# A DoRA linear layer: 4 MB blocks with results written over the input rows, in place of 2 MB blocks with output buffers of their own

## The chip, the cores and the metric

The kernel runs on one core of one Trainium2 chip. The time is the device time of one execution in microseconds (us); the figure given for a kernel is the median over several runs.

## The reference

The input x has 16 x 2048 = 32,768 rows of 256 numbers (float32, 33.6 MB), and the output has the same shape. The weight is small: W (256 x 256) plus a low-rank term, each column scaled to length m.

```python
W_adapted = W + scale * (lora_A @ lora_B)          # rank 16
W_norm = np.sqrt(np.sum(W_adapted ** 2, axis=0, keepdims=True) + 1e-8)
W_final = W_adapted / W_norm * m
y = x.reshape(-1, in_dim) @ W_final
```

## The kernel before, in words

The start builds W_final once: four small loads, matmuls for A @ B and for the column norms (L116), a square root on ScalarE (L120), and multiplications on VectorE that end in `w_final`, written in two halves by L127. This part has a raised priority.

The main loop (L134) goes over 16 blocks of 2048 rows. A block is `x_sb`, 128 partitions with DJ = 16 rows of 256 float32 each; row p*16 + j of the block lies in partition p, so a partition's share is 16 KB in one piece in memory, and a load is 128 such pieces. L53 issues it from SP. A block is worked in groups of J = 4 row slots, c = 0 to 3, so 64 groups in all (call them groups 0 to 63, and the blocks 0 to 15). One group is:

- eight 128x128 transposes on TensorE (L142) from `x_sb` into `xt_ps` in PSUM;
- one cast to bf16 on VectorE (L148) into `xt_sb`;
- eight matmuls on TensorE (L153) with 256 columns of `w_final` into `y_ps`;
- one copy on ScalarE (L160) from `y_ps` into a slice of `y_sb`.

After the last group of a block, L162 issues its store from ACT's queue, `y_sb` to the output, again 16 KB per partition.

Buffers set how far the parts may run apart: six `x_sb`, five `y_sb`, six `xt_sb`, two `xt_ps`, two `y_ps`. A load may begin when the transposes of the block that used its buffer are done; a copy into `y_sb` when the store that used that buffer is done. The order of instructions on each engine is fixed when the program is built. A scheduler sets it, with its own notion of costs and of data arriving, so the order in which transposes and result matmuls alternate on TensorE is not the order of the source: transposes are put ahead by some groups.

Of the kernel before, what the change touches and what calls it, by code (L numbers as in the profile page):

```python
# [10 lines left out]
@with_exitstack  # L11
def kernel(
    ctx: ExitStack,
    tc: tile.TileContext,
    x: bass.AP,
    W: bass.AP,
    lora_A: bass.AP,
    lora_B: bass.AP,
    m: bass.AP,
    scale: float,  # L20
    out: bass.AP,
):
    nc = tc.nc
    P = 128
    FP32 = mybir.dt.float32
    BF16 = mybir.dt.bfloat16
    AF = mybir.ActivationFunctionType
    ALU = mybir.AluOpType

    x_flat = x.flatten_outer_dims()  # L30
    out_flat = out.flatten_outer_dims()
    N, IN = x_flat.shape
    OUT = W.shape[1]
    R = lora_A.shape[1]
    KC = IN // P
    J = 4
    DJ = 16
    BLK = DJ * P
    NBLK = N // BLK

    assert IN % P == 0 and OUT % P == 0 and N % BLK == 0

    consts = ctx.enter_context(tc.tile_pool(name="consts", bufs=1))
    startup = ctx.enter_context(tc.tile_pool(name="startup", bufs=1))
    xpool = ctx.enter_context(tc.tile_pool(name="xpool", bufs=6))
    xtpool = ctx.enter_context(tc.tile_pool(name="xtpool", bufs=6))
    ypool = ctx.enter_context(tc.tile_pool(name="ypool", bufs=5))
    pp_xt = ctx.enter_context(tc.tile_pool(name="pp_xt", bufs=2, space=bass.MemoryType.PSUM))
    pp_y = ctx.enter_context(tc.tile_pool(name="pp_y", bufs=2, space=bass.MemoryType.PSUM))

    def load_x(b):
        t = xpool.tile([P, DJ, IN], FP32, name="x_sb", tag="x_sb")
        nc.sync.dma_start(  # L53
            out=t,
            in_=x_flat[b * BLK : (b + 1) * BLK].rearrange("(p j) k -> p j k", p=P),
        )
        return t


    a_nat = startup.tile([P, KC, R], FP32)  # L60
    nc.scalar.dma_start(out=a_nat, in_=lora_A.rearrange("(c p) r -> p c r", p=P))
    w_nat = startup.tile([P, KC, OUT], FP32)
    nc.sync.dma_start(out=w_nat, in_=W.rearrange("(c p) o -> p c o", p=P))  # L63
    b_nat = startup.tile([R, OUT], FP32)
    nc.scalar.dma_start(out=b_nat, in_=lora_B)
    m_row = startup.tile([1, OUT], FP32)
    nc.scalar.dma_start(out=m_row, in_=m[None, :])

    identity = consts.tile([P, P], FP32)
    make_identity(nc, identity)  # L70
    ones = consts.tile([P, P], FP32)
    nc.vector.memset(ones, 1.0)
    eps_col = startup.tile([P, 1], FP32)
    nc.vector.memset(eps_col, 1e-8)

    warm = startup.tile([P, 1], FP32)
    nc.scalar.activation(out=warm, in_=eps_col, func=AF.Sqrt)  # L77

    w_final = consts.tile([P, KC, OUT], BF16)

    with tc.high_priority():
        b_bf = startup.tile([R, OUT], BF16)
        nc.vector.tensor_copy(out=b_bf, in_=b_nat)  # L83

        aT_ps = pp_y.tile([R, KC * P], FP32, tag="psy", name="aT_ps")
        for c in range(KC):
            nc.tensor.transpose(aT_ps[:, c * P : (c + 1) * P], a_nat[:, c, :], identity)  # L87
        aT = startup.tile([R, KC * P], BF16)
        nc.vector.tensor_copy(out=aT, in_=aT_ps)  # L89

        mb_ps = pp_y.tile([P, OUT], FP32, tag="psy", name="mb_ps")
        nc.tensor.matmul(mb_ps, ones[0:1, :], m_row, start=True, stop=True)  # L92
        m_all = startup.tile([P, OUT], FP32)
        nc.vector.tensor_copy(out=m_all, in_=mb_ps)  # L94

        ab_ps = pp_y.tile([P, KC, OUT], FP32, tag="psy", name="ab_ps")
        for c in range(KC):
            nc.tensor.matmul(  # L98
                ab_ps[:, c, :],
                aT[:, c * P : (c + 1) * P],  # L100
                b_bf,
                start=True,
                stop=True,
            )

        wa = startup.tile([P, KC, OUT], FP32)
        nc.vector.scalar_tensor_tensor(  # L107
            out=wa, in0=ab_ps, scalar=float(scale), in1=w_nat, op0=ALU.mult, op1=ALU.add
        )
        sq = startup.tile([P, KC, OUT], FP32)  # L110
        nc.vector.tensor_mul(out=sq, in0=wa, in1=wa)  # L111


        n2_ps = pp_y.tile([P, OUT], FP32, tag="psy", name="n2_ps")
        for c in range(KC):
            nc.tensor.matmul(  # L116
                n2_ps, ones, sq[:, c, :], start=(c == 0), stop=(c == KC - 1)
            )
        norm = startup.tile([P, OUT], FP32)
        nc.scalar.activation(out=norm, in_=n2_ps, func=AF.Sqrt, bias=eps_col)  # L120
        wam = startup.tile([P, KC, OUT], FP32)
        for c in range(KC):
            nc.vector.tensor_mul(out=wam[:, c], in0=wa[:, c], in1=m_all)  # L123
        rnorm = startup.tile([P, OUT], FP32)
        nc.vector.reciprocal(out=rnorm, in_=norm)  # L125
        for c in range(KC):
            nc.vector.tensor_mul(out=w_final[:, c], in0=wam[:, c], in1=rnorm)  # L127

    j_order = []
    for a in range(J // 2):  # L130
        j_order.append(a)
        j_order.append(a + J // 2)

    for b in range(NBLK):  # L134
        x_sb = load_x(b)
        y_sb = ypool.tile([P, DJ, OUT], FP32, name="y_sb")

        for c in range(DJ // J):
            xt_ps = pp_xt.tile([P, KC, J * P], FP32, tag="psxt", name="xt_ps")
            for j in range(J):  # L140
                for kc in range(KC):
                    nc.tensor.transpose(  # L142
                        xt_ps[:, kc, j * P : (j + 1) * P],
                        x_sb[:, c * J + j, kc * P : (kc + 1) * P],
                        identity,
                    )
            xt_sb = xtpool.tile([P, KC, J * P], BF16, name="xt_sb")
            nc.vector.tensor_copy(out=xt_sb, in_=xt_ps)  # L148

            y_ps = pp_y.tile([P, J, OUT], FP32, tag="psy", name="y_ps")  # L150
            for kc in range(KC):
                for j in j_order:
                    nc.tensor.matmul(  # L153
                        y_ps[:, j, :],
                        xt_sb[:, kc, j * P : (j + 1) * P],
                        w_final[:, kc, :],
                        start=(kc == 0 and (j % (J // 2)) == 0),
                        stop=(kc == KC - 1 and (j % (J // 2)) == (J // 2) - 1),
                    )
            nc.scalar.copy(out=y_sb[:, c * J : (c + 1) * J, :], in_=y_ps)  # L160

        nc.scalar.dma_start(  # L162
            out=out_flat[b * BLK : (b + 1) * BLK].rearrange("(p j) k -> p j k", p=P),
            in_=y_sb,
        )


# [33 lines left out]
```

## Time and profile before

| | |
|---|---|
| median of 8 runs | 165.92 us (165.60 to 166.53) |
| the profiled execution | 166.41 us, of which its span is 164.6 us |
| HBM read and written | 33.85 MB and 33.55 MB, 409 GB/s over the span |
| TensorE busy | 128.3 us (78%) |
| VectorE busy | 81.1 us (49%) |
| ScalarE busy | 63.9 us (39%) |
| one load: issue to landing | 2 MB, median 35.6 us |
| one store: issue to landing | 2 MB, median 15.7 us, shortest 8.1 |

The profile covers the execution on one core, from the first instruction to the last. The span is less than the time of the execution, as something lies around it. The page gives busy time by engine, then rows of 40 slices in which each digit is a busy share in tenths (the DMA row is the mean over 16 DMA engines), then the DMA queues with packets, megabytes and their share of the engines' time. PE is TensorE, PEld its weight loads, DVE VectorE, ACT ScalarE. A list of stretches gives, for each, its length, the busy time of PE, PEld, DVE, ACT and POOL with the instructions in it, TensorE's granted clock, the DMA share, and GB/s. A timeline lists instructions in order: start, duration, engine, line, operation, and in square brackets how long the engine had stood idle and what ended that.

### The profile page before, as it was taken

Reading aid. Unit: us, or ns where it says so; the run is one execution under the profiler, and the core shown is the slowest. Engines: PE = TensorE matmul, PEld = TensorE weight load, DVE = VectorE, ACT = ScalarE, POOL = GpSimd, SP = SyncE. Lnnn points to the kernel's source line nnn. Section 1 sums busy time; section 2 is a strip of 40 time slices with the busy share of each in tenths; the row PEclk is TensorE's granted clock in tenths of the full one; section 3 lists DMA queues with packets and bytes.
Section 4 is the critical chain, followed back from the end, with each engine's and each line's share of the span. In section 5 each row is a group of like instructions: output and inputs, shape, how many; then the busy total and the mean of one; then the engine's idle time right before and its main releaser. Section 6 shows DMA issues by size and latency. Waiting matters only on the chain.

```text
span 164.6 us, 2402 instructions
## 1 busy us (share of the span) xinstructions
PE 128.3 (78%) x1034; PEld 110.8 (67%) x1034; DVE 81.1 (49%) x76; ACT 63.9 (39%) x67; POOL 0.7 (0%) x6
## 2 busy tenths in 40 slices
PE   0495987989989898989898986989679894998300
PEld 0174876877867878787877876778577783897200
DVE  0198457569194646564646462564605555262000
ACT  3001742350714535353531714444406353268500
POOL 1000000000000000000000000000000000000000
PEclk9999999999999999999999997899978999999975
DMA  6999999999999999999999999999999999999991
GB/s 185 400 442 442 430 414 314 442 438 406 434 438 430 418 426 442 436 422 418 438 434 426 426 430 442 420 426 426 438 438 422 418 442 434 422 414 406 426 426 84
DMA packets 5196, 67.55 MB, mean 410 GB/s; under 512 B 817, under 2 KB 1090, under 8 KB 1090
## 3 DMA queue, kind: packets, MB, share of 16 engines
q1 hardware_dynamic: 2576, 33.82, 49.1%
q10 hardware_dynamic: 2610, 33.59, 48.0%
q8 instruction: 8, 0.13, 0.3%
q14 instruction: 2, 0.02, 0.0%
HBM read 33.85 MB, written 33.55 MB: 409 GB/s over the span
## 4 chain that ended last, share of the span: by engine, by line
PE 41%; DMA 34%; DVE 9%; ACT 6%; another core or an unknown queue 1%; issue 1%; SPq 0%
DMA x_sb<-in_x_dram 34%; PE xt_ps L142 20%; PE y_ps L153 20%; DVE xt_sb L148 8%; ACT y_sb L160 6%; DVE rnorm L125 1%; PE n_ps L116 1%; ACT norm L120 0%; SPq L63 0%
## 5 line engine op out<-in xcount | busy, mean ns | idle before, releaser
L148 DVE CAST xt_sb<-xt_ps 128x1024 bf16<-128x1024 f32 x64 | 75.6, 1219 | 59.6 <-PE y_ps L153 30.7
L160 ACT COPY y_sb<-y_ps 128x1024 f32<-128x1024 f32 x64 | 61.9, 1015 | 79.7 <-PE y_ps L153 70.0
L142 PE MATMUL xt_ps<-identity,x_sb 128*128 128x128 f32 x512 | 69.9, 284 | 15.1 <-DMA x_sb<-in_x_dram 9.5
L142 PEld LDWEIGHTS xt_ps<-identity,x_sb 128*128 128x128 f32 x512 | 59.1, 146 | 21.9 <-DVE xt_sb L148 20.4
L153 PE MATMUL y_ps<-w_final,xt_sb 128*128 128x256 bf16 x512 | 64.1, 276 | 3.7 <-ACT y_sb L160 2.7
L153 PEld LDWEIGHTS <-xt_sb 128*128 128x128 bf16 x512 | 50.6, 99 | 13.2 <-issue 5.6
L120 ACT ACTIVATE norm<-n_ps,eps_col 128x256 f32<-128x256 f32 x1 | 0.5, 475 | 8.7 <-PE n_ps L116 8.7
L87 PE MATMUL aT_ps<-identity,a_nat 128*16 128x128 f32 x2 | 0.6, 394 | 4.1 <-DMA a_nat<-in_lora_A_dram 4.1
L92 PE MATMUL mb_ps<-m_row,ones 1*128 1x256 f32 x2 | 1.2, 694 | 2.4 <-DMA m_row<-in_m_dram 2.4
L87 PEld LDWEIGHTS aT_ps<-identity,a_nat 128*16 128x16 f32 x2 | 0.1, 87 | 4.0 <-issue 4.0
L83 DVE CAST b_bf<-b_nat 16x256 bf16<-16x256 f32 x1 | 0.3, 282 | 5.0 <-DMA b_nat<-in_lora_B_dram 5.0
L92 PEld LDWEIGHTS mb_ps<-m_row,ones 1*128 1x128 f32 x2 | 0.5, 304 | 2.9 <-DVE aT L89 2.9
L77 ACT ACT_TABLE_LOAD x1 | 1.3, 1283 | 2.3 <-issue 2.3
L125 DVE RECIPROCAL rnorm<-norm 128x256 f32<-128x256 f32 x1 | 1.8, 1752 | 0.8 <-ACT norm L120 0.8
L116 PE MATMUL n_ps<-sq,ones 128*128 128x256 f32 x4 | 1.5, 516 | 0.0
L94 DVE COPY m_all<-mb_ps 128x256 f32<-128x256 f32 x1 | 0.4, 425 | 1.7 <-PE mb_ps L92 1.7
L116 PEld LDWEIGHTS n_ps<-sq,ones 128*128 128x128 f32 x4 | 1.1, 310 | 0.2
L123 DVE TENSOR_TENSOR wam<-wa,m_all 128x256 f32<-128x256 f32 x2 | 0.8, 420 | 0.0
L127 DVE TENSOR_TENSOR w_final<-wam,rnorm 128x256 bf16<-128x256 f32 x2 | 0.7, 411 | 0.0
L111 DVE TENSOR_TENSOR sq<-wa 128x512 f32<-128x512 f32 x1 | 0.7, 694 | 0.0
L107 DVE SCALAR_TENSOR_TENSOR wa<-ab_ps,w_nat 128x512 f32<-128x512 f32 x1 | 0.7, 692 | 0.0
L98 PE MATMUL ab_ps<-b_bf,aT 16*128 16x256 bf16 x2 | 0.6, 416 | 0.0
(11 smaller groups left out, 2.0 us busy)
## 6 DMA issues: line engine op xcount, KB each, us to landing
x_sb<-in_x_dram SPq DMA_DIRECT2D x16, 2048.0 KB, 35.6
out_dram<-y_sb ACTq DMA_DIRECT2D x16, 2048.0 KB, 15.7
w_nat<-in_W_dram SPq DMA_DIRECT2D x1, 256.0 KB, 3.0
a_nat<-in_lora_A_dram ACTq DMA_DIRECT2D x1, 16.0 KB, 3.2
b_nat<-in_lora_B_dram ACTq DMA_DIRECT2D x1, 16.0 KB, 4.7
m_row<-in_m_dram ACTq DMA_DIRECT2D x1, 1.0 KB
```

The lines of the kernel that those rows point to most:

```text
L77: nc.scalar.activation(out=warm, in_=eps_col, func=AF.Sqrt)
L87: nc.tensor.transpose(aT_ps[:, c * P : (c + 1) * P], a_nat[:, c, :], identity)
L92: nc.tensor.matmul(mb_ps, ones[0:1, :], m_row, start=True, stop=True)
L107: nc.vector.scalar_tensor_tensor(out=wa, in0=ab_ps, scalar=float(scale), in1=w_nat, op0=ALU.mult, op1=ALU.add)
L111: nc.vector.tensor_mul(out=sq, in0=wa, in1=wa)
L116: nc.tensor.matmul(n2_ps, ones, sq[:, c, :], start=(c == 0), stop=(c == KC - 1))
L123: nc.vector.tensor_mul(out=wam[:, c], in0=wa[:, c], in1=m_all)
L125: nc.vector.reciprocal(out=rnorm, in_=norm)
L142: nc.tensor.transpose(xt_ps[:, kc, j * P : (j + 1) * P], x_sb[:, c * J + j, kc * P : (kc + 1) * P], identity,)
L148: nc.vector.tensor_copy(out=xt_sb, in_=xt_ps)
L153: nc.tensor.matmul(y_ps[:, j, :], xt_sb[:, kc, j * P : (j + 1) * P], w_final[:, kc, :], start=(kc == 0 and (j % (J // 2)) == 0), stop=(kc ...
L160: nc.scalar.copy(out=y_sb[:, c * J : (c + 1) * J, :], in_=y_ps)
```

## The change

The number of row slots per block doubles, DJ from 16 to 32, so there are 8 blocks of 4096 rows and 4 MB, a block has eight groups (c = 0 to 7), and a partition's share of a load or a store is 32 KB in one piece. The separate output buffers go. ScalarE copies a group's result into the slice of `x_sb` that held the group's input rows, and the store reads from `x_sb`. There are five of these buffers; each is held from the load to the end of the store.

```diff
     J = 4
-    DJ = 16
+    DJ = 32
     BLK = DJ * P
...
-    assert IN % P == 0 and OUT % P == 0 and N % BLK == 0
+    assert IN == OUT and IN % P == 0 and OUT % P == 0 and N % BLK == 0
...
-    xpool = ctx.enter_context(tc.tile_pool(name="xpool", bufs=6))
+    xpool = ctx.enter_context(tc.tile_pool(name="xpool", bufs=5))
     xtpool = ctx.enter_context(tc.tile_pool(name="xtpool", bufs=6))
-    ypool = ctx.enter_context(tc.tile_pool(name="ypool", bufs=5))
...
         x_sb = load_x(b)
-        y_sb = ypool.tile([P, DJ, OUT], FP32, name="y_sb")
+
...
-            nc.scalar.copy(out=y_sb[:, c * J : (c + 1) * J, :], in_=y_ps)
+            nc.scalar.copy(out=x_sb[:, c * J : (c + 1) * J, :], in_=y_ps)
...
         nc.scalar.dma_start(
             out=out_flat[b * BLK : (b + 1) * BLK].rearrange("(p j) k -> p j k", p=P),
-            in_=y_sb,
+            in_=x_sb,
         )
```

## The prediction

> **What bounds the kernel now.** I read the page's rows of slices and queues first, then busy time by stretch, then the chain of waits at its end, then the timeline of TensorE and of the ACT queue there. From parts 2 and 3 of the page:
>
> ```profile
> PE   0495987989989898989898986989679894998300
> ...
> DMA  6999999999999999999999999999999999999991
> ...
> q1 hardware_dynamic: 2576, 33.82, 49.1%
> q10 hardware_dynamic: 2610, 33.59, 48.0%
> ```
>
> The DMA row is at 9 from the second slice to the last but one, while TensorE, the busiest engine, falls to 4 and 6 late in the run. The queues share alike: q1 (loads, from SP) and q10 (stores, from ACT). So the bytes set the time. The next view, stretches of time, has the DMA share and GB/s in its last two columns:
>
> ```profile
> 25.00:29.00 4.00, 3.26 (x28) 2.95 (x29) 3.12 (x4) 1.01 (x1) 0.00 (x0) 1.00 0.96 287
> 35.00:140.00 105.00, 90.36 (x741) 78.69 (x738) 57.76 (x49) 43.18 (x45) 0.00 (x0) 0.97 1.01 430
> 140.00:150.00 10.00, 9.55 (x85) 8.61 (x86) 4.71 (x4) 5.40 (x6) 0.00 (x0) 1.00 0.99 421
> 150.00:152.00 2.00, 1.81 (x18) 1.43 (x16) 0.00 (x0) 1.79 (x3) 0.00 (x0) 1.00 0.83 352
> 152.00:161.00 9.00, 1.60 (x15) 1.15 (x12) 0.00 (x0) 2.45 (x3) 0.00 (x0) 0.88 1.01 431
> ```
>
> 430 GB/s is the plateau, whether loads run alone (431 from 8 to 23 us), stores alone (431 from 152 on) or both. Two holes stand out: 25 to 29 us, where the first store's packets come in, loses (430-287) x 4 us = 572 KB, 1.3 us; 150 to 152 us loses (430-352) x 2 = 156 KB, 0.36 us. The account closes: 2.0 us until data flows, 67.4 MB at 430 GB/s = 156.7, the two holes 1.7, slow small loads up to 8 us (393 GB/s) 0.5, and 140 to 150 us 0.2, make 161.1; the last data is seen at about 161.2, and 3.4 us remain until the end of the span, 164.6.
>
> The second hole is explained by the tail, here in the timeline:
>
> ```profile
> 139.98 1.94 PE L142 MATMUL xt_ps<-identity,x_sb 128*128 128x128 f32 x16 [2.36 <-DMA x_sb<-in_x_dram]
> 141.76 1.91 PE L153 MATMUL y_ps<-w_final,xt_sb 128*128 128x256 bf16 x16
> ...
> 145.75 1.80 PE L142 MATMUL xt_ps<-identity,x_sb 128*128 128x128 f32 x15
> 147.38 1.91 PE L153 MATMUL y_ps<-w_final,xt_sb 128*128 128x256 bf16 x16
> 149.52 1.95 PE L153 MATMUL y_ps<-w_final,xt_sb 128*128 128x256 bf16 x16 [0.23 <-ACT y_sb L160]
> 151.66 1.95 PE L153 MATMUL y_ps<-w_final,xt_sb 128*128 128x256 bf16 x16 [0.18 <-ACT y_sb L160]
> ```
> ```profile
> 150.60 0.34 ACTq L162 DMA_DIRECT2D out_dram<-y_sb  x1
> 154.68 0.34 ACTq L162 DMA_DIRECT2D out_dram<-y_sb  x1
> ```
>
> The last load lands at 139.85. After it TensorE still has 4 groups of transposes (8 each) and **10** groups of result matmuls, since matmuls run 6 groups behind transposes in its fixed order. The tail takes 14.7 us, and store 14 comes out at 150.60, a moment after store 13 has drained. Counting back from 161.2 by two stores of 4.88 us (2.097 MB at 430), its data began at 151.4: 0.8 us from issue to data, 0.36 of it with empty queues.
>
> **What the skill says.** "DMA: Bandwidth & Descriptors", Where 436 GB/s comes from, gives a ceiling of 435 GB/s; the 430 here is 99% of it. Its section Queues, rings and completion order says that an engine alternates between queues packet by packet, so equal packets share equally; the shares from 35 to 140 us, 49.1% and 51.4%, agree. Why small descriptors are slow puts a fixed 3 cycles on each packet; for 16 KB (512 beats of 32 B) that is an estimate of 0.6%, and no row here isolates it. Latency and other measured facts tells of a loss at large power-of-two row pitches, from 512 KiB on (207 against 214 GB/s); the pitch grows here from 16 to 32 KB, and no run shows what that does.
>
> **The change part by part.**
>
> Descriptors: 4096 packets of 16 KB become 2048 of 32 KB; bytes stay. If the whole gap to 435 (67.1 MB: 156.1 against 154.3 us, 1.8) were per packet, halving saves 0.9 us; with the 3 cycles it is 0.3% or 0.5; the other end is the pitch, for which I allow 0.5 lost. I take 0, since nothing in the trace says that the 1% is per packet. Half the DMA issues go (16 to 8 each way); at 0.33 us on sequencers they cost nothing, as loads are queued far ahead.
>
> First load: lands at 9.03 + 2.097 MB/431 = 13.9 instead of 9.03. Transposes before w_final (ready about 16.6) were 27 by 16.5 us, 3.4 groups. From 14.0, paced by casts of 1.22, some 1.7 groups fit: 1.7 x 1.09 = 1.8 us of TensorE lost. The norm matmuls at L116, behind nine transposes now (9.08 to 11.26), come up to 1.1 earlier; so 0.7 to 1.8 and I keep 1.8. The DMA hides it: it runs on queued loads.
>
> First store: eight groups instead of four. The second store of before was issued at 33.40; + 1.8 is 35.2. In the trace of before the first store's packets came 4.2 us after the issue; so sharing starts at 39.4 instead of 27.5.
>
> Loads after that go at 215 GB/s. Before: from 27.5 to 139.85, 24.2 MB, so 9.4 MB were in by 27.5. After: 9.4 + 11.9 x 0.43 = 14.5 MB by 39.4, and the other 19.05 MB take 88.6 us: the last load lands at **128.0**.
>
> Shared buffers: load b+5 now waits for store b, where before the transposes freed x. Queued behind that wait on SP are only later loads. Store 0 takes 4.19/0.215 = 19.5 us, done about 61.3 with 2.4 of completion (the shortest store's 8.1 less 0.8 and 4.88); loads 0 to 4 last until 39.4 + 6.5/0.215 = 69.6. A cover of 8 us, and the same for loads 6 and 7. Cost 0; were it gone, the stores would take the full rate meanwhile, and the last load would come later. The evictions (61.9 us for 64) lose their wait on y buffers and write slices that were already transposed; 0.
>
> Tail: steady pace is 8.29 us for 4 groups (57.01 to 65.30). TensorE began block 9's transposes at 81.89, so group 56 could begin at 81.9 + 1.8 + 5 x 8.29 = 125.2; the data come at 128.0. From there 8.3 for four groups, then the same 14.7: the last store is issued at **151.0**, the one before (4.8 us after the 14.7 begin) at 141.1. Without gaps the data of before would have ended at 161.2 - 0.36 = 160.8; a 4 MB store takes 9.75, so store 5 would drain at 141.3, store 6 at 151.1. Store 6's data come at 141.9 (gap 0.6), end at 151.65; store 7's at 151.8 (0.15), end at 161.6. So 0.75 of gaps in place of 0.36: **+0.4 us**.
>
> Opening hole: 1.3 us, whose cause the trace doesn't name; if it is a count of packets in flight it doubles (+1.3), if of bytes it stays, and it may be a little less. I take it unchanged.
>
> Sum: span 164.6 + 0.4; the profiled execution, 166.41 (1.8 outside its span), would be 166.8. It lies 0.5 above the median; on the median 165.92 + 0.4 = 166.3. Within 0.2% (165.6 to 166.25) a measurement can't tell it from no change.
>
> **The rivals.**
> - *Tail as reckoned* (0.40), 165.9 to 167.2, likeliest 166.3.
> - *Faster*: 32 KB packets carry less overhead, and the order of work comes out with matmuls closer behind transposes, so that the tail has no gap (0.32). For it: 1% to the ceiling is there, and early (16 us) the lag is under 4 groups. Against: loads and stores alone and mixed give the same rate. 165.92 - 0.36 - 0.9 = 164.7; with half the gain or some gap, 165.5. It decides when the rate from 35 us on passes 432.
> - *Nothing left or lost* (0.15): no gap, rate as before: 165.6.
> - *A late tail or a doubled opening hole* (0.12): if the lag is 8 groups throughout, or the pace 8.7 per four, the last store slips to 153 or 154: 168 to 170; the doubled hole alone 167.6.
> - *In-place writes held against transposes* (0.01): if the wait were on a whole buffer, each group would chain transposes, cast, matmuls and eviction, 1.09 + 1.22 + 0.9 + 1.02 = 4.2 us, 64 times: 280 us. Against it: parts of one buffer are told apart now, as the first result matmul (16.36) starts while w_final's second half is written (two writes, 15.84 to 16.58):
>
> ```profile
> 15.84 0.74 DVE L127 TENSOR_TENSOR w_final<-wam,rnorm 128x256 bf16<-128x256 f32 x2
> 16.36 1.91 PE L153 MATMUL y_ps<-w_final,xt_sb 128*128 128x256 bf16 x16
> ```
>
> **How the numbers follow.** Slower by over 0.2%: 0.32 of the first case, 0.12, 0.01 = 0.45. Same: 0.08 of the first, 0.06 of the second, 0.09 of the third = 0.23. Faster: 0.26 + 0.06 = 0.32. The range runs from the full packet gain to a moderately late tail, 164.6 to 168.4; the likeliest case's own is 165.9 to 167.2.
>
> **What would show it.** First store issued near 35; last load landing near 128; the last two stores near 141 and 151; GB/s 430 in the middle. A middle above 432 shows the packet gain; a last store after 152 with a dip before it the late tail; a first-store hole well over 0.6 MB the doubled one. The forecast fails if the DMA rate moves by 0.5%, which is more than the tail's term.

## The result and the profile after

| | before | after |
|---|---|---|
| median | 165.92 us | 167.16 us |
| profiled execution / its span | 166.41 / 164.6 us | 167.18 / 165.3 us |
| GB/s, 50 to 110 us | 429 | 435 |
| last load landed | 139.9 | 129.4 |
| last two stores issued | 150.60, 154.68 | 138.83, 153.09 |
| last store landed | 163.6 | 164.2 |

The ratio of after to before is 1.0066, 95% interval 1.0056 to 1.0076, which is 1.1 us; the medians differ by 1.24 us. The kernel became slower, inside the range and on the side forecast, but by three times the 0.4 us reckoned. (The profiled execution of before lies 0.5 us above its median, that of after on it; so the two spans differ by 0.7 only.) Ratios here leave out the few executions that fell in a slower state of the chip, medians don't, which matters only for experiment 7 and its repeat (170.13 and 169.90 us without them).

Parts 1 to 3 of the page of after:

```profile
span 165.3 us, 2364 instructions
...
PE   0059888888999889988998999888998799797000
...
DMA  5999999999999989999999998999989999991885
...
q1 hardware_dynamic: 1424, 33.82, 48.2%
q10 hardware_dynamic: 1458, 33.59, 47.4%
```

The bytes are the same, and half as many packets carry x and the output, in less queue time than before (49.1 and 48.0% of a slightly shorter span). But the DMA row has a 1 near its end, when all loads are in and only stores are left to move. Busy time by stretch, of after (DMA share and GB/s last):

```profile
33.00:50.00 17.00, 15.39 (x126) 12.88 (x125) 11.78 (x10) 5.94 (x7) 0.00 (x0) 1.00 0.98 400
50.00:110.00 60.00, 55.20 (x455) 46.39 (x455) 32.11 (x28) 29.64 (x30) 0.00 (x0) 1.00 1.01 435
52.00:112.00 60.00, 55.16 (x453) 46.31 (x451) 34.06 (x29) 27.78 (x28) 0.00 (x0) 1.00 0.99 428
...
150.00:152.00 2.00, 1.81 (x16) 1.25 (x13) 0.00 (x0) 1.85 (x2) 0.00 (x0) 1.00 0.07 25
150.00:154.00 4.00, 1.83 (x16) 1.25 (x13) 0.00 (x0) 2.86 (x3) 0.00 (x0) 1.00 0.19 78
152.00:161.00 9.00, 0.02 (x1) 0.00 (x0) 0.00 (x0) 1.01 (x1) 0.00 (x0) 0.62 0.82 350
```

and stretches of before that were not shown yet:

```profile
22.00:40.00 18.00, 16.39 (x139) 14.16 (x136) 12.00 (x11) 6.89 (x7) 0.00 (x0) 1.00 1.00 400
50.00:110.00 60.00, 53.02 (x440) 46.60 (x439) 31.84 (x28) 26.98 (x28) 0.00 (x0) 0.97 1.01 429
52.00:112.00 60.00, 52.73 (x438) 46.40 (x436) 32.83 (x28) 26.83 (x28) 0.00 (x0) 0.97 1.01 430
```

Three things are to be read from this. First, the plateau. From 50 to 110 us it seems to rise from 429 to 435, but the view counts a whole packet at its start, and 16 packets of 32 KB, which start close together, are 0.5 MB, or 9 GB/s of a 60 us stretch. Two microseconds later the same stretch holds 428 in after and 430 in before. So these rows don't show a faster stream; that takes the experiments. Second, the hole at the first store. By the rows it is (430-400) x 18 = 540 KB in before and (430-400) x 17 = 510 KB in after, again with 0.5 MB of doubt in after; with the bytes of each packet spread over the packet's own time it is 0.49 and 0.32 MB. It did not double. Third, and far beyond such doubt, hardly any data moves from 150 to 154 us, until the last store starts. What TensorE and ACT's queue did then, in the timeline of after:

```profile
129.57 1.94 PE L141 MATMUL xt_ps<-identity,x_sb 128*128 128x128 f32 x16 [1.23 <-DMA x_sb<-in_x_dram]
131.35 1.91 PE L152 MATMUL y_ps<-w_final,xt_sb 128*128 128x256 bf16 x16
...
144.65 2.22 PE L141 MATMUL xt_ps<-identity,x_sb 128*128 128x128 f32 x16 [0.45 <-DVE xt_sb L147]
146.71 1.91 PE L152 MATMUL y_ps<-w_final,xt_sb 128*128 128x256 bf16 x16
148.85 1.95 PE L152 MATMUL y_ps<-w_final,xt_sb 128*128 128x256 bf16 x16 [0.23 <-ACT x_sb L159]
150.98 1.03 PE L152 MATMUL y_ps<-w_final,xt_sb 128*128 128x256 bf16 x8 [0.19 <-ACT x_sb L159]
```
```profile
138.83 0.34 ACTq L161 DMA_DIRECT2D out_dram<-x_sb  x1
153.09 0.34 ACTq L161 DMA_DIRECT2D out_dram<-x_sb  x1
```

The last load is in at 129.4, and the work on it, from 129.57 to the issue of the last store, takes 23.5 us. The second-last store had moved nearly all its data by 151, and the last, all 4 MB of it, could not be issued before 153.09. By their landings these two are 11.5 us apart (152.7 and 164.2), where a 4 MB store takes 9.8 at 430 GB/s. By this estimate the end is 1.7 us later than with a full queue.

### The profile page after: what moved, and what is told of

Same layout as the page of the kernel before. It is cut to its first block, busy times and chain, and to the rows that moved or that the text cites. A ratio compares the mean times of both kernels' runs of the same rounds, so it can differ in the third digit from the quotient of the medians.

```text
span 165.3 us, 2364 instructions
## 1 busy us (share of the span) xinstructions
PE 129.8 (79%) x1034; PEld 108.5 (66%) x1034; DVE 81.3 (49%) x76; ACT 65.6 (40%) x67; POOL 0.7 (0%) x6
## 4 chain that ended last, share of the span: by engine, by line
DMA 40%; PE 34%; DVE 12%; ACT 4%; issue 1%; ACTq 1%; SPq 0%
PE y_ps L152 20%; DMA x_sb<-in_x_dram 19%; DMA out_dram<-x_sb 17%; PE xt_ps L141 12%; DVE xt_sb L147 10%; DMA m_row<-in_m_dram 4%; ACT x_sb L159 4%; PE n_ps L115 1%; DVE rnorm L124 1%; PE mb_ps L91 1%; DVE w_final L126 0%; DVE sq L110 0%; DVE wa L106 0%; ACTq L64 0%; ACTq L60 0%
## 5 line engine op out<-in xcount | busy, mean ns | idle before, releaser
L159 ACT COPY x_sb<-y_ps 128x1024 f32<-128x1024 f32 x64 | 63.6, 1013 | 75.1 <-PE y_ps L152 72.8
L141 PE MATMUL xt_ps<-identity,x_sb 128*128 128x128 f32 x512 | 71.7, 281 | 7.0 <-DVE xt_sb L147 5.2
L141 PEld LDWEIGHTS xt_ps<-identity,x_sb 128*128 128x128 f32 x512 | 58.2, 144 | 15.9 <-DVE xt_sb L147 13.3
L152 PEld LDWEIGHTS <-xt_sb 128*128 128x128 bf16 x512 | 49.2, 97 | 16.2 <-DVE xt_sb L147 5.7
L115 PE MATMUL n_ps<-sq,ones 128*128 128x256 f32 x4 | 2.1, 674 | 1.5 <-DVE sq L110 1.5
```

The lines of the kernel that those rows point to most:

```text
L115: nc.tensor.matmul(n2_ps, ones, sq[:, c, :], start=(c == 0), stop=(c == KC - 1))
L141: nc.tensor.transpose(xt_ps[:, kc, j * P : (j + 1) * P], x_sb[:, c * J + j, kc * P : (kc + 1) * P], identity,)
L152: nc.tensor.matmul(y_ps[:, j, :], xt_sb[:, kc, j * P : (j + 1) * P], w_final[:, kc, :], start=(kc == 0 and (j % (J // 2)) == 0), stop=(kc ...
L159: nc.scalar.copy(out=x_sb[:, c * J : (c + 1) * J, :], in_=y_ps)
```

## The experiments

The experiments have numbers. The letters in the expectations name theories.

**1. The block size undone, the in-place writes kept.**

```diff
-    DJ = 32
+    DJ = 16
-    xpool = ... bufs=5
+    xpool = ... bufs=10
```

> In-place writes kept, block back to 2 MB with 16 KB pieces, ten shared buffers. Theory A (two terms: larger pieces save about 2.4 us of data time, a late last store costs about 2 to 3 us): both terms leave, load-to-load spacing returns to 9.8 us per 2 MB, time 165.6 to 166.3. Rival B (the in-place buffers, held from load to end of store, are what costs): time stays at 167 or above.

165.98 us, ratio to before 1.000 (0.9988 to 1.0012), as theory A said. In the place of before's hole at 150 us the queue is full:

```profile
150.00:152.00 2.00, 1.82 (x17) 1.44 (x15) 0.00 (x0) 1.80 (x3) 0.00 (x0) 1.00 1.02 434
```

Shared buffers and in-place writes cost nothing that this comparison can see, to 0.2 us; what changed the time comes with the block size. One thing remains odd: before's hole of 0.36 us is gone and the time is the same. So either that hole cost nothing, or something as small took its place; no run separates the two.

**2. 4 MB transfers cut into 16 KB pieces**, two per partition, in loads and (not shown) stores alike.

```diff
-            out=t,
-            in_=x_flat[...].rearrange("(p j) k -> p j k", p=P),
+            out=t.rearrange("p (h j) k -> p h j k", h=2),
+            in_=x_flat[...].rearrange("(h p j) k -> p h j k", h=2, p=P),
```

> The changed kernel with each 4 MB transfer cut into 16 KB pieces (two per partition). Theory A with the piece size as the cause of the faster stream: spacing of loads goes from 19.35 to 19.6 us or more, last load lands 1.5 to 2 us later, time 168.5 to 169.3. Rival C (fewer, larger transfers, each with one set of completions, are what made the stream faster): spacing stays at 19.35, time 167.2.

167.43 us, ratio to before 1.0076 (1.0047 to 1.0106). The last load lands at 129.6, not 1.5 to 2 us later, so theory A's 2.4 us for the pieces is out as their price. In the traces, 4 MB of loads land 19.44 us apart (four intervals), against 19.37 with 32 KB pieces and 19.65 before. But experiment 1, with 2 MB transfers, has 19.45 too (two of its intervals) in all places but one. And where loads and stores don't share equally (49.1 against 51.4% of the engines' time in before, 48.4 against 51.9% in experiment 1, from 35 to 140 us), the interval of the loads is not the rate of the stream. So the 19.65 doesn't show a cost of smaller transfers. With a hole at the end that depends on when the queue drains, the times of such kernels don't add, so I went on to the transfers alone.

**3. The last block stored in two halves**, the first after its fourth group; all other transfers stay 4 MB.

```diff
+            if b == NBLK - 1 and c % 4 == 3:
+                nc.scalar.dma_start(out=...[:, (c - 3) * J : (c + 1) * J, :],
+                                    in_=x_sb[:, (c - 3) * J : (c + 1) * J, :])
-        nc.scalar.dma_start(... in_=x_sb)
+        if b < NBLK - 1:
+            nc.scalar.dma_start(... in_=x_sb)
```

> The changed kernel with only the last block's store issued in two 2 MB halves (16 KB pieces), the first after its fourth group. Theory A: the queue of stores no longer runs empty before the end; the data gap of 3 us near 150 us closes to under 0.5 us, time 164.2 to 165.5, below the kernel before. Rival D (the gap only absorbs engines that lag anyway, so the slowest engine sets the end): time 166.5 to 167.2.

165.24 us, ratio to before 0.996 (0.9942 to 0.9978): 1.92 us less than the changed kernel and the fastest version that does the whole work. Its last stores, the stretch that held 25 GB/s, and its end:

```profile
138.79 0.34 ACTq L170 DMA_DIRECT2D out_dram<-x_sb  x1
148.79 0.34 ACTq L162 DMA_DIRECT2D out_dram<-x_sb  x1
153.26 0.34 ACTq L162 DMA_DIRECT2D out_dram<-x_sb  x1
```
```profile
150.00:152.00 2.00, 1.77 (x16) 1.45 (x15) 0.00 (x0) 1.79 (x3) 0.00 (x0) 1.00 0.83 344
159.00:160.00 1.00, 0.00 (x0) 0.00 (x0) 0.00 (x0) 0.00 (x0) 0.00 (x0) 0.50 0.65 279
160.00:162.00 2.00, 0.00 (x0) 0.00 (x0) 0.00 (x0) 0.00 (x0) 0.00 (x0) 0.50 0.16 66
```

The work ends no earlier (153.26); 2 MB of it is merely queued by 148.79, before the store ahead drains. So the late last store is the cause, and its price is 1.9 us by the medians (1.8 by the ratios). The gap itself is longer: 78 GB/s from 150 to 154 us leave 3.3 us' worth of data out. Part of it is made good at the end, where experiment 3 falls to 279 and 66 GB/s while its slowest pieces come in, and the changed kernel's last sixteen pieces all start within 0.2 us (162.47 to 162.62). Rival D, that the gap absorbs engines that lag anyway, is thus out as the whole account and fits a part of it.

**4. Three `xt_sb` buffers instead of six**, for a smaller lag.

```diff
-    xtpool = ... bufs=6
+    xtpool = ... bufs=3
```

> The changed kernel with three instead of six bf16 buffers between transposes and result matmuls, so that matmuls can lag by three to five groups only. Theory A (the tail is eight groups of transposes plus the lag): last store issued about 2 to 3 us earlier after the last landing than the 23.5 us of the changed kernel, time 164.8 to 166.2. Rival D: the gap shrinks but the time stays within 0.3 us of 167.2. If TensorE instead becomes slower for lack of buffers, the last store is later and the time above 167.5.

165.65 us, ratio 0.9979 (0.9964 to 0.9994). The time is as expected, the reason isn't: from the last landing (128.25) to the last store it took 23.6 us, as in the changed kernel (from 129.44). What came earlier is the landing itself, by 1.2 us, and the last store with it (151.89). TensorE now works without a wait for that load; its last two stores are 16.7 us apart, eight groups at its own pace of 2.09. The 1.2 us is already there when the fourth load lands, at 50.8 instead of 52.0, while the first store was issued at 34.1 instead of 33.9. Why stays open. What the run does show is the dose: last store 1.2 us sooner, landings of the last two stores 10.3 instead of 11.5 us apart, time 1.5 us shorter.

**5. Transfers alone**, four kernels with the arithmetic left out, each block stored as it was loaded.

> Transfers alone: weights, transposes, matmuls and copies are left out, each loaded block is stored as it is (the output is x). 2 MB transfers, 16 KB pieces, ten buffers. Theory E (each finished transfer costs every DMA engine about 0.1 us) and theory F (pieces of 16 KB cost against 32 KB): the slowest of three, load-to-load spacing 9.8 us per 2 MB load and 2 MB store, as in the full kernel. If the stream of the full kernel was slowed by compute instead: spacing near 9.65 here too.

> Transfers alone (arithmetic left out, output is x), 4 MB transfers in 16 KB pieces, five buffers. Theory E: about 16 x 0.1 = 1.6 us shorter than the 2 MB copy, as short as the copy with 32 KB pieces within 0.4 us. Theory F: no shorter than the 2 MB copy.

> Transfers alone (arithmetic left out, output is x), 4 MB transfers in 32 KB pieces, five buffers. Theory E: 1.6 to 2.0 us shorter than the 2 MB copy, within 0.4 us of the one with 4 MB and 16 KB. Theory F: about 2 us shorter than both others.

> Transfers alone (arithmetic left out, output is x), 2 MB transfers in 8 KB pieces, ten buffers. Theory E: within 0.6 us of the copy with 2 MB and 16 KB. Theory F (a fixed cost per piece, which doubles again): about 4 us longer than it.

| transfer, piece | packets | median us | ratio to before |
|---|---|---|---|
| 2 MB, 8 KB | 8704 | 163.68 | 0.9858 (0.9835 to 0.9881) |
| 2 MB, 16 KB | 4608 | 162.85 | 0.9817 (0.9785 to 0.9849) |
| 4 MB, 16 KB | 4352 | 162.33 | 0.9779 (0.9754 to 0.9803) |
| 4 MB, 32 KB | 2304 | 161.94 | 0.9759 (0.9734 to 0.9784) |

Neither theory came out in its size. By the medians, 4096 fewer pieces cost 0.83 us less and 2048 fewer 0.39 less; over 16 engines that is 3.2 and 3.0 ns a piece. 16 fewer transfers went with 0.52 us less. The intervals of neighbours overlap, so the single steps are less sure than their order. The traces say more. From 20 to 140 us, in the order of the table (the last three columns are TensorE's clock, the DMA share and GB/s, as before; of the engines only POOL is listed):

```profile
20.00:140.00 120.00, 0.00 (x0) 1.00 1.01 428
20.00:140.00 120.00, 0.00 (x0) 1.00 1.01 431
20.00:140.00 120.00, 0.00 (x0) 1.00 1.01 432
20.00:140.00 120.00, 0.00 (x0) 1.00 1.00 433
```

The landings are sharper: from the second load to the last, 4 MB take 19.600, 19.451, 19.438 and 19.363 us. So a cost per piece is there in the stream, 4.6 and 4.7 ns of an engine's time by these intervals. A cost per transfer is not: half as many transfers change the interval by 0.013 us, some 6 ns each, which is 0.1 of the 0.52 us. The rest lies elsewhere; about 0.2 us is there as soon as the first 2 MB are in (8.35 with 2 MB loads; with 4 MB, 13.03 less the 4.87 that 2 MB take at 431 GB/s), and why isn't shown.

**6. Experiments 2 and 3 together**: 4 MB, 16 KB pieces, last store in halves.

> 4 MB blocks in 16 KB pieces, the last block stored in two 2 MB halves: the kernel without the late last store, between the run with 2 MB in place (165.98) and the split last store with 32 KB pieces (165.24). From the copies: 0.52 us less than the first for the transfers, 0.39 more than the second for the pieces, so 165.4 to 165.7. If only the piece size matters: 166.0. If only the transfer size matters: 165.2.

165.63 us, ratio 0.9989 (0.9972 to 1.0005), as worked out from the copies. Without the late last store, the ladder in the full kernel is 165.98 (2 MB, 16 KB), 165.63 (4 MB, 16 KB), 165.24 (4 MB, 32 KB): steps of 0.35 and 0.39. The two ends of the ladder have intervals apart (0.9988 to 1.0012 and 0.9942 to 0.9978), so the whole gain of 0.74 us is shown. The middle overlaps both, so how it splits into transfers and pieces is likely, not shown.

**7. The first load in two halves**, to start TensorE as early as before.

```diff
+        step = DJ // 2 if b == 0 else DJ
+        for j0 in range(0, DJ, step):
+            nc.sync.dma_start(out=t[:, j0 : j0 + step, :], in_=src[:, j0 : j0 + step, :])
```

> The changed kernel with only the first block loaded as two transfers of 2 MB, so that transposes can begin near 9 us as before instead of 13.9. Theory A (what makes the last store late is the length of the last block's tail after its landing, 23.5 us): TensorE starts 4 to 5 us earlier but waits more for the last load; last store issued 152.5 to 154, time 166.9 to 167.6. Rival G (the late start of the work is passed on to the end): last store 1.5 to 4 us earlier, time 165.3 to 166.2.

170.48 us, ratio 1.0234 (1.0193 to 1.0274), about 3 us slower than the changed kernel. Both theories missed. TensorE did start at 8.83, and the first store came 2.2 us sooner. In order: the first store, TensorE around the last load, the last two stores, and the row of granted clocks.

```profile
31.70 0.38 ACTq L161 DMA_DIRECT2D out_dram<-x_sb  x1
```
```profile
126.71 1.09 PE L141 MATMUL xt_ps<-identity,x_sb 128*128 128x128 f32 x8 [0.19 <-DVE xt_sb L147]
131.22 3.41 PE L141 MATMUL xt_ps<-identity,x_sb 128*128 128x128 f32 x16 [3.42 <-DMA x_sb<-in_x_dram]
```
```profile
141.95 0.34 ACTq L161 DMA_DIRECT2D out_dram<-x_sb  x1
156.21 0.34 ACTq L161 DMA_DIRECT2D out_dram<-x_sb  x1
```
```profile
PEclk9999999999999999999999999999999599999755
```

The last load landed at 131.1, 1.6 us later than in the changed kernel; TensorE stood 3.4 us, and its next 16 transposes took 3.41 us instead of 1.94, the row of granted clocks being at 5 there. The last two stores came 3.1 us later each, and the queue ran dry ahead of both. That an early first store delays the last load fits the rates: loads have 430 GB/s until the stores come in and half of it from then on, so each microsecond sooner should put the last load one later. By that, 2.2 us would be expected. But experiment 4 moved the last landing by 1.2 us with hardly another first store, so this isn't all of it, and I didn't isolate it: two further kernels were to hold block 0's store back.

> The changed kernel with only block 0's store issued later, after block 1's second group (near 48 us instead of 34). Theory H (the loads' head start before the first store sets when the last load lands): the last load lands 4 to 7 us earlier (122 to 126 instead of 129.4), TensorE no longer waits 1.2 us for it, last store issued near 152 instead of 153.1, time 165.8 to 166.6. Rival: holding a store back only lengthens the backlog: 167.2 or more.

> The run with the first load in two halves (170.48 us) with only block 0's store issued later, after block 1's second group (near 45 us instead of 31.7). Theory H: last load lands 6 to 9 us earlier than the 131.1 of that run, TensorE's waits for loads (6.8 us) go, last store issued 148 to 150, before the store ahead of it has drained, so no gap: time 165.0 to 165.6, below the kernel before with whole 4 MB stores. Rival (the split load itself, or the cut clock of TensorE, is what made that run slow): 168 or more.

Their edit moved the call for block 0's store to after block 1's second group. It did not take effect: the scheduler issued it at 33.90 and 31.78, where it was ready. So they repeat the changed kernel (167.45 us, ratio 1.0066, 1.0041 to 1.0091) and experiment 7 (170.67 us, 1.0221, 1.0171 to 1.0271), and say nothing of the theory. As repeats they agree: last landings 130.0 and 131.1.

## Why the prediction came out as it did

**The bound** was right: bytes at a plateau, in both kernels.

**In-place writes and shared buffers at 0**: right. Experiment 1 shows it, and load 5 was issued at 59.5, 12 us before load 4 landed (71.3); the cover was put at 8.

**First load** at 13.9: measured 13.9. **First store** at 35.2: 33.86, as in after TensorE built up its lag of six groups only after the first block. **Opening hole** unchanged: it did not double, which is as much as the views can tell.

**Descriptors at 0**: this step failed, on the faster side. I had an estimate of 0.3%, 0.5 us, from the Trainium skill's 3 cycles per packet ("DMA: Bandwidth & Descriptors", Why small descriptors are slow) and set it aside, since nothing in the trace said that the missing 1% was per packet; under the faster rival I held the one rate of loads, stores and their mixture against it. But all three had 16 KB pieces, so that comparison could not show a cost per piece. The copies gave 0.39 us, experiments 6 and 3 again 0.39, so the estimate was about right. And I costed half the transfers at nothing by looking at the issuing queues only; 0.35 to 0.52 us go with them, most of it not in the stream. The whole gain is 0.74 us, within the allowed 0.9.

**Tail**: mechanism right, size wrong. The reckoning put the last load at 128.0, the last store 23.0 us later at 151.0, and a drained queue at 151.65: a gap of 0.15. Measured: 129.4, the last store 23.6 later at 153.09, and a queue nearly drained by 151. Each term was off by 0.6 to 1.4 us, all in one direction. The first store accounts for the last load: with 33.86 in place of 35.2 in the prediction's own sum, it comes at 129.3 (experiment 4 shows, though, that the landing can also move without the first store). The queue emptied sooner also because the other gap of the reckoning, 0.6 us ahead of the second-last store, did not come: that store was issued at 138.83, not 141.1. A difference of two large times, 151.8 and 151.65, carries the errors of both. I held it to tenths; it was worth 1.9 us.

In medians the change splits into -0.74 us (experiment 3 less experiment 1) and +1.92 (after less experiment 3). These add up to the difference of after and experiment 1 by their making, so the sum confirms nothing; that each part is real rests on the intervals. That the forecast lay so near is luck in part: two mis-sized terms of opposite sign, -0.74 in place of 0 and +1.9 in place of 0.4, partly cancelled. By its own sign, a last store after 152 with a dip before it, what came was the late tail, to which it gave 0.12. That rival's numbers (168 to 170) were too high for the changed kernel, since they left out the gain. The faster rival was half right: the gain of its packets exists, but the tail took it back. Its sign, a middle above 432, can't be read from one row, as said above; from 45 to 125 us the rows hold 429 in before and 431 in after, and the copies 431 and 433, just under the 0.5% at which the forecast was to fail.

## What to carry to other kernels

When the DMA queues are full throughout, as here, larger blocks may save only little per byte and make the last block's work and its store longer: check that the last store is issued before the one ahead has drained, and if not, store the last block in parts. Both limits of the last store, TensorE's own pace from a late start and the last landing plus its tail, should be worked out, as relieving one exposes the other. Don't take an equal rate of loads and stores as evidence that pieces cost nothing; vary the piece. Don't read a rate off one stretch when a handful of packets at its edges is as large as the difference; shift the stretch, or take the intervals of the landings.

## What was not expected of the hardware

A piece cost some 3 ns of a DMA engine's time by the medians of the copies and 4.6 by their landings, between 8 and 32 KB; a transfer cost next to nothing beyond its pieces in the stream (some 6 ns). A gap of 3.3 us in the data near the end cost 1.9 us of time. Starting TensorE 5 us earlier made the kernel about 3 us slower.

After a wait of 3.4 us for a load, TensorE ran 16 transposes in 3.41 us instead of 1.94 with its granted clock at half; after 1.2 us (after) and 2.1 us (experiment 7) it didn't. But no length of the wait divides the cases. Before has this row, while a wait of 2.36 us there (at 139.98, shown in the prediction) was followed by 1.94:

```profile
100.39 3.34 PE L142 MATMUL xt_ps<-identity,x_sb 128*128 128x128 f32 x16 [2.21 <-DMA x_sb<-in_x_dram]
```
